# Six of eight modulation blocks summed over input tiles on VectorE, ScalarE and GpSimd instead of TensorE

## The chip, the cores and the metric

The kernel runs on one core of a Trainium2 chip. The time is that of the device for one execution, in microseconds; the median of several runs counts. The engines are TensorE (PE in the profile, PEld its weight loads), VectorE (DVE), ScalarE (ACT) and GpSimd (POOL); SyncE (SP) issues most DMAs. Each engine works through a queue of its own in order, and they wait for each other by semaphores.

## The reference

Two layers over a latent stream `x` (1024 tokens x 1024) and a context `ctx` (256 tokens x 1024): a windowed attention with sinks and rotary positions, then a bidirectional state-space mixer. Ahead of each mixer the stream is normalized and modulated, behind it the result is gated. What the change touches is where shift, scale and gate come from:

```python
def adaln(cond, w, b):
    mod = jax.nn.silu(cond) @ w + b
    return jnp.split(mod, 3, axis=-1)

for i in range(DEPTH):                       # 2 layers
    shift, scale, gate = adaln(c, w_ada[i], b_ada[i])
    shift_c, scale_c, gate_c = adaln(c_ctx, w_ada[i], b_ada[i])
    u = rms_normalize(h) * (1.0 + scale[:, None]) + shift[:, None]
    ...
    h = h + gate[:, None] * y
```

For each layer this is a product of two rows (c and c_ctx after silu) of length 1024 with a matrix of 1024 x 3072, plus a bias. All data are float32.

## The kernel before

**Modulation.** The matrix of a layer is cut into six column blocks of 512 (blocks 0 and 1 shift, 2 and 3 scale, 4 and 5 gate), and each block into eight input tiles of 128 rows, 128 x 512 in SBUF. Blocks 0 to 3 of layer 0 are needed at once and come first (`ada0`, L361). The eight others, (0,4), (0,5) and (1,0) to (1,5), are needed only later. `adaln_col` (L172) makes nine steps of each: step k loads tile k (L181, buffers `wh` and `wl` of the pool wv, four each); steps 3 and 7 add four float32 matmuls (L185) with 32 output columns each, one to each quarter of the PSUM tile `aps`. The weights `cs` hold the two rows in columns 0 and 1, zeros in the other 30, so partitions 32j and 32j + 1 hold the partial sums of the tiles j and 4 + j. The ninth step copies the PSUM tile to SBUF (L189) and calls `modulation` (L196): four matmuls against `sel`, two columns (L201), add up the four quarters and turn the row of 512 into four columns of 128 partitions; VectorE adds the bias (L203) into the tile `mod`. A float32 matmul is carried out in two passes, so the profile counts twice the instructions.

**The stage around it.** `qkvg` (L551) projects the modulated stream to k, v, q and g. Each product is done in three matmuls, with the operands split into a high part and a low part (`mm3`, L223, matmuls at L227 to L229). First come k and v for the three token tiles `TT` (512, 512 and 256 tokens), then eight column tiles x of wq, then eight of wg. For each x two halves of the weights (128 x 512) are loaded into `wr` (seven buffers, L220), split by ScalarE into `wh` (L213) and by VectorE into `wl` (L215), four buffers each, so the split runs one x ahead. Then follow the projections of the context tile (24 matmuls of 256 columns) and of the first latent tile (24 of 512); for the first four x of wg the latent tile was done earlier, and only the context tile is left. Results land in one of four PSUM tiles `pj`. q goes through `rope` (L496): VectorE reads PSUM twice (L501, L502), GpSimd multiplies by the sine (L503), VectorE adds (L504), ScalarE and VectorE split the sum (L522, L523) and SyncE stores it; the context tile of q is split from PSUM (L525, L526). g is read by ScalarE (L541) and VectorE (L542).

**What sets the order.** After each projection `fill` runs two or three of the 72 modulation steps, in the order in which the program is written:

```python
n = [3, 3, 3, 2]
for x in range(8):
    w = self.load_halves(a["wq"][x])
    for i in (2, 0):
        self.q_step(p, w, x, i)
        fill(n[x % 2 * 2 + (i == 0)])
```

The framework schedules the instructions of each engine from there by a time estimate of its own; the queues that result are fixed when the program is built. Behind the stage its pools are closed, and `attention` (L686) takes their memory; it interleaves the attention of the blocks with what is left of the projections. The gate of layer 0 is read in the output projection there (L724), the blocks of layer 1 later.

Of the kernel before, what the change touches and what calls it, by code (L numbers as in the profile page):

```python
# [17 lines left out]
P = 128  # L18
D = 1024
KT = D // P  # L20
# [22 lines left out]
    pj=1, S=2, pt=2, pv=1,  # L43
# [14 lines left out]
POST = 0.5  # L58
LATE = 3.0
DTLATE = (10.0, 13.0)  # L60
SEGS = (1.5, 2.0, 2.0, 2.2, 2.2)
_STOP = None

# [40 lines left out]
class Kernel:  # L104
# [52 lines left out]
    def load_cond(self, p):  # L157
        nc, t, cp = self.nc, self.t, self.cp
        cc = t(p, [P, KT, 2], F32, "cc")
        nc.sync.dma_start(cc, self.a["cc"].rearrange("p (k c) -> p k c", k=KT))  # L160
        th = t(p, [P, KT, 2], F32, "cth")
        nc.scalar.activation(th, cc, AF.Tanh, scale=0.5)
        nc.vector.tensor_scalar_mul(cc, cc, 0.5)
        cs = self.csf = t(cp, [P, KT, 2], F32, "cs")
        nc.vector.scalar_tensor_tensor(cs, in0=th, scalar=1.0, in1=cc, op0=ALU.add, op1=ALU.mult)

        self.sel = t(cp, [P, 2], F32, "sel")
        nc.vector.tensor_reduce(self.sel, self.ident.rearrange("p (j r) -> p r j", r=32)[:, 0:2], axis=mybir.AxisListType.X, op=ALU.add)
        self.bada = t(cp, [P, 2, 24], F32, "bada")
        nc.sync.dma_start(self.bada, self.a["bada"].rearrange("p (l t) -> p l t", l=2))  # L170

    def adaln_col(self, layer, n, pool, ps):  # L172

        nc, t = self.nc, self.t
        st = {}

        def step(k):
            if k == 0:
                st["ps"] = t(ps, [P, 512], F32, "aps", 2)
            raw = t(pool, [P, 4, P], F32, ("wh", "wl")[k // 4])  # L180
            nc.sync.dma_start(raw, self.a["w_ada"][layer, n, k].rearrange("p (a c) -> p a c", a=4))  # L181
            st[k] = raw
            if k % 4 == 3:
                for j in range(4):
                    nc.tensor.matmul(st["ps"][32 * j : 32 * j + 32], self.cs[:, k - 3 + j, :], st[k - 3 + j].rearrange("p a c -> p (a c)"), start=k == 3, stop=k == KT - 1)  # L185

        def fin():
            row = t(self.pq, [P, 512], F32, "qf")
            nc.scalar.copy(row, st["ps"])  # L189
            m = self.modulation(layer, n, row, ps)  # L190
            if n // 2 == 2 and layer == 0:
                nc.vector.tensor_scalar_mul(m, m, 0.5)

        return [lambda k=k: step(k) for k in range(KT)] + [fin]

    def modulation(self, layer, n, row, ps):  # L196

        nc = self.nc
        mt = self.t(ps, [P, 512], F32, "pt")
        for j in range(4):  # L200
            self.last_mod = nc.tensor.matmul(mt[:, 2 * j : 2 * j + 2], row[:, j * P : (j + 1) * P], self.sel, start=True, stop=True)  # L201
# [96 lines left out]
    def layer0(self):  # L298
        nc, t, a = self.nc, self.t, self.a
        cps = ExitStack()  # L300
        BUFS.update(S=1, pj=4, wr=7, qf=2, ql=2, wh=4, wl=4, sqt=2)
        self.psA = self.pool("psA", space=PSUM, ctx=cps)
        NB = (LAT + CTX) // P
        self.uH, self.uL = [None] * 3, [None] * 3
        cw = ExitStack()
        wvp = self.pool("wv", ctx=cw)

        self.cs = t(wvp, [P, KT, 32], F32, "cs32")
        nc.vector.memset(self.cs, 0.0)
        nc.vector.tensor_copy(self.cs[:, :, 0:2], self.csf)  # L310
# [12 lines left out]
        self.mask = t(kvp, [P, 1152], BF16, "mask")  # L323
        self.nsink = t(kvp, [P, HEADS], F32, "nsink")
        self.sink = t(kvp, [P, HEADS], F32, "sink")
        self.qkvg(p, wk, wv, wvp)
        if "u" in self.dump:
            for i, (s, n) in enumerate(TT):
                self.dump_split("u", self.uH[i], self.uL[i], i, n, s)
        cw.close()  # L330
        cps.close()
        with ExitStack() as c1:
            BUFS.update(S=2, pj=1)
            self.psA = self.pool("psT", space=PSUM, ctx=c1)
            self.attention(c1, ckv)
            BUFS.update(pj=2)
# [24 lines left out]
    def ada0(self, n, raw, ps):  # L361

        nc, t = self.nc, self.t
        pj = t(ps, [P, 512], F32, "aps", 2)
        for k in range(KT):
            j = k % 4
            mm = nc.tensor.matmul(pj[32 * j : 32 * j + 32], self.cs[:, k, :], raw[k // 2][:, k % 2], start=k < 4, stop=k >= 4)
# [128 lines left out]
    def rope(self, pool, ps, i, out):  # L496
        nc = self.nc
        s, n = TT[i]
        b = self.t(pool, [P, 512], F32, "rope_b")
        s -= self.rope_o  # L500
        nc.vector.tensor_mul(out, ps, self.cos[:, s : s + n])  # L501
        nc.vector.stream_shuffle(b, ps, mask=[(j + 16) % 32 for j in range(32)])  # L502
        nc.gpsimd.tensor_tensor(b, b, self.sin[:, s : s + n], op=ALU.mult)  # L503
        nc.vector.tensor_add(out, out, b)  # L504

    def load_rope(self, p, s, n):
        self.rope_o = s
        self.cos = self.t(p, [P, n], F32, "cos")
        self.sin = self.t(p, [P, n], F32, "sin")
        self.nc.sync.dma_start(self.cos, self.a["cos"][:, s : s + n])  # L510
        self.nc.sync.dma_start(self.sin, self.a["sin"][:, s : s + n])

    def qk(self, p, pj, i, l=None):
        nc, t = self.nc, self.t
# [36 lines left out]
    def qkvg(self, p, wk, wv, wvp):  # L551
        nc, t, a = self.nc, self.t, self.a
        ps = self.psA
# [3 lines left out]
        v = self.v  # L557
# [21 lines left out]
        for i, (s, n) in enumerate(TT):  # L579
# [22 lines left out]
        for x in range(8):  # L602
            w = self.load_halves(a["wg"][x])
# [354 lines left out]
    def dt_tail(self, raw, post):  # L958
# [153 lines left out]
    def ssd(self, c0):  # L1112
# [194 lines left out]
        with ExitStack():  # L1307
            for g in range(G):
# [321 lines left out]
```

## Time and profile before

| | us |
|---|---|
| median of 3 runs | 1850.06 (1848.47 to 1850.49) |
| the profiled execution | 1852.09 |
| its span, first to last instruction | 1850.4 |
| TensorE busy in the span | 1764.7 (95%) |
| VectorE, ScalarE, GpSimd busy | 1171.9, 894.8, 803.8 |
| first and last L185 matmul of the eight blocks | 142.6, 264.3 |

The last g matmul of the stage starts at 273.9 us, and attention follows. A matmul's row shows its own duration; since matmuls overlap in the array, the distance from one start to the next is what it costs the queue. Where rows are quoted, the columns of the timeline are start, duration, engine, line, operation, tiles (output<-inputs), shape, count and, in brackets, the idle time before with what ended it; the columns of a group are count, busy time, mean duration in ns and the idle time before. A row by line gives the shortest, median and longest duration in ns, and the first and last start.

### The profile page before, as it was taken

How to read it: one execution, taken by the hardware profiler on the slowest of the kernel's cores; microseconds unless marked ns; L12 is line 12 of the kernel's file. 1: busy time of each engine (PE TensorE's matmuls, PEld its weight loads, DVE VectorE, ACT ScalarE, POOL GpSimd, SP SyncE). 2: the span in 40 equal slices, each digit the busy share in tenths (PEclk: the TensorE clock that was granted, in tenths of full speed). 3: DMA queues.
4: the chain of work that ended last, by engine and by line, in shares of the span. 5: the costliest groups of instructions: out<-in, count | busy, mean ns of one | idle time of the engine just before them, and what ended most of it. 6: DMA issues, size and time to landing. Idle time of an engine off the chain costs nothing. (4 is left out here: it accounts for less than half of the span.)

```text
span 1850.4 us, 29176 instructions
## 1 busy us (share of the span) xinstructions
PE 1764.7 (95%) x10375; PEld 1506.2 (81%) x10375; DVE 1171.9 (63%) x2144; ACT 894.8 (48%) x1963; POOL 803.8 (43%) x1066
## 2 busy tenths in 40 slices
PE   6899998899999999989999999999999999999997
PEld 2697776788889687768889898988989898888886
DVE  4534426887777755684776757676675767766643
ACT  3812226677778765573443535344353534454422
POOL 2331107654456454202454554545455454554321
PEclk8999999999999999999999999999999999999998
DMA  8658856553355455321332333332232323455542
GB/s 313 233 135 254 250 160 150 132 124 88 95 129 131 105 147 169 127 67 43 83 74 78 81 77 78 80 89 69 77 93 65 86 72 99 150 170 166 177 137 69
DMA packets 212498, 227.64 MB, mean 123 GB/s; under 512 B 16384, under 2 KB 149632, under 8 KB 212352
## 3 DMA queue, kind: packets, MB, share of 16 engines
q1 hardware_dynamic: 178288, 207.12, 37.7%
q0 software_dynamic: 34064, 18.65, 5.6%
q8 instruction: 82, 1.34, 0.3%
q14 instruction: 64, 0.52, 0.1%
HBM read 190.88 MB, written 35.13 MB: 122 GB/s over the span
## 5 line engine op out<-in xcount | busy, mean ns | idle before, releaser
L227 PE MATMUL pj<-uH,wh 128*128 128x512 f32 (+1 forms) x712 | 257.7, 363 | 18.4 <-ACT uH L446 8.5
L228 PE MATMUL pj<-uL,wh 128*128 128x512 f32 (+1 forms) x712 | 244.9, 344 | 0.2 <-DVE uL L447 0.2
L229 PE MATMUL pj<-uH,wl 128*128 128x512 f32 (+1 forms) x712 | 244.2, 344 | 0.7 <-POOL wl L215 0.5
L1140 POOL TENSOR_TENSOR xw<-xn,dtdec 128x256 f32<-128x256 f32 x144 | 106.3, 741 | 197.2 <-PE psD L1165 125.0
L227 PEld LDWEIGHTS pj<-uH,wh 128*128 128x128 f32 x712 | 136.4, 192 | 48.1 <-issue 10.3
L1071 PE MATMUL pj<-uH,wh 128*128 128x512 f32 x512 | 165.6, 399 | 4.4 <-ACT bn L1025 2.4
L1071 PE MATMUL pj<-uL,wh 128*128 128x512 f32 x512 | 167.8, 401 | 1.1 <-DVE uL L291 1.1
L1071 PE MATMUL pj<-uH,wl 128*128 128x512 f32 x512 | 167.2, 401 | 0.7 <-DVE wl L1002 0.7
L215 POOL TENSOR_TENSOR wl<-wr,wh 128x512 fp32r<-128x512 f32 x92 | 123.0, 1341 | 88.3 <-ACT wh L213 87.8
L666 DVE TENSOR_TENSOR pl<-pt,ph 128x512 fp32r<-128x512 f32 x168 | 114.4, 687 | 66.3 <-ACT ph L665 65.5
L1096 PE MATMUL pj<-wh,uH 128*128 128x256 f32 x512 | 151.0, 295 | 2.6 <-ACT xn L1025 2.6
L228 PEld LDWEIGHTS pj<-uL,wh 128*128 128x128 f32 x712 | 137.0, 192 | 15.9 <-DVE uL L447 2.5
L229 PEld LDWEIGHTS pj<-uH,wl 128*128 128x128 f32 x712 | 135.9, 191 | 17.1 <-POOL wl L215 2.0
L1096 PE MATMUL pj<-wh,uL 128*128 128x256 f32 x512 | 149.1, 291 | 0.0
L1096 PE MATMUL pj<-wl,uH 128*128 128x256 f32 x512 | 146.4, 286 | 0.0
L213 ACT CAST wh<-wr 128x512 fp32r<-128x512 f32 (+1 forms) x132 | 84.7, 645 | 115.7 <-PE pj L228 83.2
L640 DVE CUSTOM_DVE_ANT_0 sm<-S,mask,nsink 128x640 f32<-128x640 f32 (+2 forms) x160 | 119.2, 771 | 21.4 <-PE S L637 13.6
L665 ACT CAST ph<-pt 128x512 fp32r<-128x512 f32 x168 | 97.4, 585 | 58.9 <-PE pt L661 55.3
L642 ACT ACTIVATE sm<-sm,nm 128x640 f32<-128x640 f32 (+2 forms) x160 | 118.7, 742 | 12.4 <-DVE nm L640 12.0
L1071 PEld LDWEIGHTS pj<-uH,wh 128*128 128x128 f32 x512 | 94.7, 189 | 25.0 <-ACT bn L1025 2.6
L1071 PEld LDWEIGHTS pj<-uL,wh 128*128 128x128 f32 x512 | 96.6, 189 | 21.9 <-DVE uL L291 2.0
L1071 PEld LDWEIGHTS pj<-uH,wl 128*128 128x128 f32 x512 | 96.4, 189 | 20.5 <-DVE wl L1002 1.1
(370 smaller groups left out, 4821.8 us busy)
## 6 DMA issues: line engine op xcount, KB each, us to landing
wr<-w_x SPq DMA_DIRECT2D x32, 512.0 KB, 5.2
M<-acs SPq DMA_DIRECT2D x64, 256.0 KB, 5.1
bw<-acs SPq DMA_DIRECT2D x64, 256.0 KB, 5.0
wr<-wo SPq DMA_DIRECT2D x48, 256.0 KB, 2.7
wr<-w_sk SPq DMA_DIRECT2D x24, 512.0 KB, 4.5
wr<-wg SPq DMA_DIRECT2D x40, 256.0 KB, 3.7
qs<-q POOLq DMA_DIRECT2D x40, 256.0 KB, 3.8
wada<-w_ada SPq DMA_DIRECT2D x16, 512.0 KB, 7.4
```

Source lines behind the costliest of these rows:

```text
L213: nc.scalar.copy(h, raw)
L215: (eng or nc.vector).tensor_tensor(l, raw, h, op=ALU.subtract)
L227: self.nc.tensor.matmul(ps, lh, rh, start=first and i == 0, stop=False)
L228: self.nc.tensor.matmul(ps, lh, rl, start=False, stop=False)
L229: self.nc.tensor.matmul(ps, ll, rh, start=False, stop=last and i == n - 1)
L640: nc.vector.tensor_tensor_reduce(out=sm[:, :W], in0=Sv, in1=self.mask[:, m0 : m0 + W], scale=-SCALE, scalar=self.nsink[:, 4 * j + r : 4 * ...
L642: nc.scalar.activation(sm[:, :W], sm[:, :W], AF.Exp, bias=nm[:, r : r + 1], scale=-1.0, accum_out=sums[:, r : r + 1])
L665: nc.scalar.copy(ph, ptf)
L666: nc.vector.tensor_sub(pl, ptf, ph)
L1071: nc.tensor.matmul(raw[:, 512 * i : 512 * i + 512], l[:, k, :], r[i][:, k, :], start=k + y == 0, stop=k == KT - 1 and y == 2)
L1096: nc.tensor.matmul(pj[:, c], l, r[:, k, :], start=c % 2 + q + k + y == 0, stop=c % 2 == 1 and q == 1 and k == 3 and y == 2)
L1140: nc.gpsimd.tensor_tensor(xw, X(st, c).rearrange("p (r h) -> p r h", r=R), self.dtdec[:, c, hd(d, g)].unsqueeze(2).broadcast_to([P, R, HP] ...
```

## The change

Six of the eight blocks, (0,4), (0,5) and (1,0) to (1,3), are summed over their eight input tiles by other engines: for row 0 VectorE computes `acc0 = tile * c0 + acc0` with c0 a value per partition; for row 1 ScalarE multiplies the tile in place by c1 and GpSimd adds it to `acc1`. What is left for TensorE is the sum over the 128 partitions: four matmuls of 256 columns for a block against `pick`, a tile of zeros with a column of ones, which puts the result of block i at partition 32g + i of one PSUM tile for all six. The other two, (1,4) and (1,5), stay on TensorE, and share a PSUM tile too: their place in it is set by where the window of 32 columns is put on `cs`, now 34 wide. At the end each of the two PSUM tiles is copied and turned once (24 and 4 columns), instead of one turn for each block.

The order of the blocks is one sum, one whole, five sums, one whole. There are 72 steps, as before: step s loads tile s, uses tile s - 2, and adds the total of a block four steps after its last use; the last two turn. The tiles load into six buffers: the four `wl`, and the second halves of the rope tables, which are now loaded as two halves each (`cos0`, `cos1`, `sin0`, `sin1`) and whose second halves are free once k is projected. The four `wh` hold two pairs of accumulators. The rest of the kernel is the same in the program; the scheduler's order differs from there to about 130 us into the attention.

```diff
-        self.sel = t(cp, [P, 2], F32, "sel")
+        self.sel = t(cp, [P, 4], F32, "sel")
...
-    def adaln_col(self, layer, n, pool, ps):
+    def ada1(self, p, ps):
...
+        sums = [(0, 4), (0, 5), (1, 0), (1, 1), (1, 2), (1, 3)]
+        whole = [(1, 4), (1, 5)]
+        order = [sums[0], whole[0]] + sums[1:] + [whole[1]]
+        raws, acc = {}, {}
+        aps = [t(ps, [P, 512], F32, "aps", 2) for _ in range(2)]
...
+        def load(s):
+            y, k = divmod(s, KT)
+            layer, n = order[y]
+            r = s % 6
+            raws[s] = t(p, [P, 512], F32, "wl") if r < 4 else t(self.pq, [P, 512], F32, ("cos1", "sin1")[r - 4])
+            nc.sync.dma_start(raws[s], self.a["w_ada"][layer, n, k])
+
+        def use(s):
+            y, k = divmod(s, KT)
+            x = order[y]
+            if x in whole:
+                if k % 4 == 3:
+                    i = whole.index(x)
+                    for j in reversed(range(4)):
+                        nc.tensor.matmul(aps[1][32 * j : 32 * j + 32], self.cs[:, k - 3 + j, 2 - 2 * i : 34 - 2 * i], raws.pop(s - 3 + j), start=i == 0 and k == 3, stop=i == 1 and k == KT - 1)
+                return
+            raw = raws.pop(s)
+            c0, c1 = self.csf[:, k, 0:1], self.csf[:, k, 1:2]
             if k == 0:
+                acc[x] = [t(p, [P, 512], F32, "wh") for _ in range(2)]
+                nc.vector.tensor_scalar(out=acc[x][0], in0=raw, scalar1=c0, scalar2=None, op0=ALU.mult)
+                nc.scalar.activation(acc[x][1], raw, AF.Copy, scale=c1)
+            else:
+                nc.vector.scalar_tensor_tensor(acc[x][0], in0=raw, scalar=c0, in1=acc[x][0], op0=ALU.mult, op1=ALU.add)
+                nc.scalar.activation(raw, raw, AF.Copy, scale=c1)
+                nc.gpsimd.tensor_tensor(acc[x][1], acc[x][1], raw, op=ALU.add)
+
+        def total(x):
+            i = sums.index(x)
+            a = acc.pop(x)
+            for g in reversed(range(4)):
+                nc.tensor.matmul(aps[0][32 * g : 32 * g + 32, :256], self.pick[:, 5 - i : 37 - i], a[g // 2][:, g % 2 * 256 : g % 2 * 256 + 256], start=i == 0, stop=i == 5)
+
+        def turn(b, w):
+            row = t(self.pq, [P, 512], F32, "qf")[:, :w]
+            nc.scalar.copy(row, aps[b][:, :w])
+            m = mt[b] = t(ps, [P, 512], F32, "pt")
+            sel = self.sel if b else self.ident.rearrange("p (g r) -> p g r", r=32)[:, :, 0:6]
+            n = 4 if b else 24
+            for j in range(w // P):
+                nc.tensor.matmul(m[:, n * j : n * j + n], row[:, j * P : (j + 1) * P], sel, start=True, stop=True)
...
+        def step(s):
+            if s < 8 * KT:
+                load(s)
+            if 0 <= s - LOOK < 8 * KT:
+                use(s - LOOK)
+            y, k = divmod(s - LOOK - LAGS, KT)
+            if k == KT - 1 and y >= 0 and order[y] in sums:
+                total(order[y])
+
+        steps = [lambda s=s: step(s) for s in range(8 * KT + LOOK + LAGS)]
+        return steps + [fin_sums, fin_whole]
...
-        self.cs = t(wvp, [P, KT, 32], F32, "cs32")
+        self.cs = t(wvp, [P, KT, 34], F32, "cs34")
...
+        self.pick = t(wvp, [P, 37], F32, "pick")
...
     def load_rope(self, p, s, n):
...
+        for h in range(n // 512):
+            for table, name in ((self.cos, "cos"), (self.sin, "sin")):
+                table.append(self.t(p, [P, 512], F32, f"{name}{h}"))
+                self.nc.sync.dma_start(table[h], self.a[name][:, s + 512 * h : s + 512 * h + 512])
...
-        ada = []
-        for layer, n in [(0, 4), (0, 5)] + [(1, n) for n in range(6)]:
-            ada += self.adaln_col(layer, n, wvp, ps)
+        ada = self.ada1(wvp, ps)
```

`LOOK` is 2 and `LAGS` is 4. `fin_sums` and `fin_whole` turn the two tiles and add the biases on VectorE.

More of the change, by code (lines that the diff above doesn't have):

```diff
@@ L60 @@
 DTLATE = (10.0, 13.0)
+LOOK = 2
+LAGS = 4
 SEGS = (1.5, 2.0, 2.0, 2.2, 2.2)
@@ L170, in load_cond, with fin_whole, fin_sums @@
         nc.sync.dma_start(self.bada, self.a["bada"].rearrange("p (l t) -> p l t", l=2))
-    def adaln_col(self, layer, n, pool, ps):
+    def ada1(self, p, ps):
         nc, t = self.nc, self.t
-        st = {}
-        def step(k):
-            if k == 0:
[L179 to L194, printed above, removed]
+        sums = [(0, 4), (0, 5), (1, 0), (1, 1), (1, 2), (1, 3)]
[3 more added lines that the diff above has]
+        aps = [t(ps, [P, 512], F32, "aps", 2) for _ in range(2)]
+        mt = {}
+        def load(s):
[15 more added lines that the diff above has]
+            c0, c1 = self.csf[:, k, 0:1], self.csf[:, k, 1:2]
+            if k == 0:
+                acc[x] = [t(p, [P, 512], F32, "wh") for _ in range(2)]
[18 more added lines that the diff above has]
+                nc.tensor.matmul(m[:, n * j : n * j + n], row[:, j * P : (j + 1) * P], sel, start=True, stop=True)
+        def fin_whole():
+            turn(1, 512)
+            nc.vector.tensor_tensor(self.mod[1][:, 16:24].rearrange("p (n j) c -> p n j c", j=4), mt[1][:, :16].rearrange("p (j n c) -> p n j c", n=2, c=2),
+                                    self.bada[:, 1, 16:24].rearrange("p (n j) -> p n j", j=4).unsqueeze(3).broadcast_to([P, 2, 4, 2]), op=ALU.add)
+        def fin_sums():
+            turn(0, 256)
+            v = mt[0][:, :48].rearrange("p (j c h n) -> p c n h j", j=2, c=2, h=2)
+            for layer, n0, n1, i in ((0, 4, 6, 0), (1, 0, 4, 2)):
+                for c in range(2):
+                    nc.vector.tensor_tensor(self.mod[layer].rearrange("p (n h j) c -> p c n h j", h=2, j=2)[:, c, n0:n1], v[:, c, i : i + n1 - n0],
+                                            self.bada[:, layer, 4 * n0 : 4 * n1].rearrange("p (n h j) -> p n h j", h=2, j=2), op=ALU.add)
+            nc.vector.tensor_scalar_mul(self.mod[0][:, 16:24], self.mod[0][:, 16:24], 0.5)
+            nc.vector.tensor_scalar_add(self.mod[1][:, 8:16], self.mod[1][:, 8:16], 1.0)
+        def step(s):
[8 more added lines that the diff above has]
+        return steps + [fin_sums, fin_whole]
@@ L200, in modulation @@
         for j in range(4):
-            self.last_mod = nc.tensor.matmul(mt[:, 2 * j : 2 * j + 2], row[:, j * P : (j + 1) * P], self.sel, start=True, stop=True)
+            self.last_mod = nc.tensor.matmul(mt[:, 2 * j : 2 * j + 2], row[:, j * P : (j + 1) * P], self.sel[:, :2], start=True, stop=True)
         m = self.mod[layer][:, n * 4 : n * 4 + 4, :]
@@ L366, in ada0 @@
             j = k % 4
-            mm = nc.tensor.matmul(pj[32 * j : 32 * j + 32], self.cs[:, k, :], raw[k // 2][:, k % 2], start=k < 4, stop=k >= 4)
+            mm = nc.tensor.matmul(pj[32 * j : 32 * j + 32], self.cs[:, k, 2:34], raw[k // 2][:, k % 2], start=k < 4, stop=k >= 4)
         row = t(self.p0, [P, 512], F32, "arow")
```

17 lines of the change are left out of this document (9 added, 8 removed).

## The prediction

> **What bounds the kernel now.** I read the page first, then the busy time in windows of the projection stage, the groups of the lines that the change touches, and the timeline of TensorE around one of them.
>
> ```profile
> span 1850.4 us, 29176 instructions
> PE 1764.7 (95%) x10375; PEld 1506.2 (81%) x10375; DVE 1171.9 (63%) x2144; ACT 894.8 (48%) x1963; POOL 803.8 (43%) x1066
> ```
> ```profile
> core 0: us, PE busy (x) PEld busy (x) DVE busy (x) ACT busy (x) POOL busy (x), PEclk, DMA share, GB/s
> 130.00:150.00 20.00, 20.00 (x135) 16.57 (x134) 5.77 (x12) 3.84 (x8) 4.80 (x8) 1.00 0.90 268
> ...
> 210.00:230.00 20.00, 20.00 (x142) 15.24 (x135) 10.21 (x20) 7.76 (x15) 1.57 (x1) 1.00 0.87 262
> ...
> 250.00:270.00 20.00, 20.00 (x121) 15.36 (x120) 4.33 (x10) 3.73 (x8) 2.81 (x4) 1.00 0.36 78
> ```
> All eight blocks are computed here, between 134 and 274 us, among the q and g projections. TensorE is busy the whole of every window at clock 1.00, VectorE about half or less, GpSimd less than a quarter: TensorE's queue sets this stage's length, and every microsecond taken from it would come off the end, if nothing else becomes late. The profiled execution took 1852.09 us (span 1850.4 and 1.7 around it), 2.0 over the median of the runs, 1850.06; differences below are applied to the median.
>
> **The change, part by part. What TensorE loses.**
> ```profile
> L185 PE MATMUL aps<-wh,cs x64: 592/605/617, 142.6 to 254.8; 128*32 128x512 f32 x64
> L185 PE MATMUL aps<-wl,cs x64: 592/605/617, 146.7 to 264.3; 128*32 128x512 f32 x64
> L201 PE MATMUL pt<-sel,qf x64: 165/251/272, 152.8 to 268.7; 128*128 128x2 f32 x64
> ```
> ```profile
> 134.17 0.28 PE L227 MATMUL pj<-uH,wh 128*128 128x256 f32 x1
> ...
> 141.61 0.39 PE L229 MATMUL pj<-uH,wl 128*128 128x512 f32 x1
> 141.84 0.39 PE L227 MATMUL pj<-uH,wh 128*128 128x512 f32 x1
> ...
> 142.29 0.39 PE L229 MATMUL pj<-uH,wl 128*128 128x512 f32 x1
> 142.61 1.07 PE L185 MATMUL aps<-wh,cs 128*32 128x512 f32 x8
> 143.61 0.39 PE L227 MATMUL pj<-uH,wh 128*128 128x256 f32 x1
> 143.83 0.28 PE L228 MATMUL pj<-uL,wh 128*128 128x256 f32 x1
> 143.95 0.29 PE L229 MATMUL pj<-uH,wl 128*128 128x256 f32 x1
> ...
> 152.58 0.39 PE L227 MATMUL pj<-uH,wh 128*128 128x512 f32 x1
> 152.81 0.95 PE L201 MATMUL pt<-sel,qf 128*128 128x2 f32 x8
> 153.62 0.49 PE L228 MATMUL pj<-uL,wh 128*128 128x512 f32 x1
> 153.94 0.40 PE L229 MATMUL pj<-uH,wl 128*128 128x512 f32 x1
> ```
> Matmuls overlap, so I price by starts. A 512-wide projection matmul starts 0.228 us after the one before, a 256-wide one 0.12. Without the group of eight, the second 256-wide one would start at 142.29 + 0.228 + 0.12 = 142.64; it starts at 143.83. So one group of four column blocks (two passes each) costs **1.19 us**, and there are 16. A turn: L229 starts 1.36 after L227 instead of 0.456, so **0.91**, eight times. Together 16 x 1.19 + 8 x 0.91 = 26.3 us.
>
> What is added: four groups for the two whole blocks, 4.8; six totals, half as wide. No row has that width; they lie between half a group, 0.6, and a whole one, 1.19. In a group the second pass follows about 1.07 - 0.605 = 0.465 after the first, so half the width saves about 0.43: I take 0.76, 4.6 in all. Two turns, one of them half as long: 0.9 + 0.5. Sum 10.8. TensorE alone: **26.3 - 10.8 = 15.5 us less.**
>
> **What the other engines gain.** 48 VectorE operations of 128x512 (42 with both tensors in SBUF), 48 on ScalarE, 42 adds on GpSimd.
> ```profile
> L215 POOL TENSOR_TENSOR wl<-wr,wh 128x512 fp32r<-128x512 f32 x92 | 123.0, 1341 | 88.3 <-ACT wh L213 87.8
> L732 POOL TENSOR_TENSOR sqa<-sqa,ut 128x512 f32<-128x512 f32 x7 | 9.1, 1296 | 0.0
> L542 DVE SCALAR_TENSOR_TENSOR qf<-qf,pj 128x512 f32<-128x512 f32 x14 | 9.6, 684 | 14.3 <-ACT qf L541 14.3
> L213 ACT CAST wh<-wr 128x512 fp32r<-128x512 f32 x124 | 76.4, 619 | 90.8 <-PE pj L228 66.9 <-DMA wr<-wo 7.7 <-DMA wr<-wq 5.9
> L289 ACT ACTIVATE h1k<-h1k,mod 128x512 f32<-128x512 f32 x8 | 6.3, 811 | 0.2 <-DVE h1k L288 0.2
> ```
> By busy time there is room on each: 42 x 1.30 = 55 us of GpSimd, 48 x 0.69 = 33 of VectorE, 48 x 0.62 to 0.81 = 30 to 39 of ScalarE, in 120 us. But GpSimd and VectorE don't run beside each other when both read two SBUF tensors:
> ```profile
> 143.97 0.67 DVE L215 TENSOR_TENSOR wl<-wr,wh 128x512 fp32r<-128x512 f32 x1
> 144.22 1.56 POOL L503 TENSOR_TENSOR rope_b<-rope_b,sin 128x512 f32<-128x512 f32 x1 [8.82 <-DVE rope_b L502]
> ...
> 218.02 1.57 POOL L503 TENSOR_TENSOR rope_b<-rope_b,sin 128x512 f32<-128x512 f32 x1 [8.86 <-DMA wh<-w_ada]
> ```
> ```profile
> 743.21 1.30 POOL L215 TENSOR_TENSOR wl<-wr,wh 128x512 fp32r<-128x512 f32 x1 [1.42 <-ACT wh L213]
> 743.27 1.79 DVE L291 TENSOR_TENSOR uL<-h,uH 128x512 fp32r<-128x512 f32 x1
> ```
> In the first pair VectorE is first and ends at 144.64; GpSimd ends at 145.78, 1.14 later. In the second GpSimd is first and ends at 744.51; VectorE ends at 745.06, 0.55 later, after 1.79 instead of 0.68. They take turns, and a turn costs **0.55 for VectorE and 1.14 for GpSimd, 1.69 a pair**. The Trainium skill (SBUF — State Buffer, section "SBUF: two separate sides") says that the shared port pair is an exclusive lock, held for the whole instruction. Where it differs is the size: whole instructions would be 0.69 + 1.30 = 1.99 a pair, while the rows show that about 0.3 of each pair overlaps. By the page's wording the sum below would come out near the upper end.
>
> **The sum.** The built order (the order of each queue as the scheduler left it, without times) puts the sums' VectorE operations among the wl splits (L215) that TensorE needs. VectorE runs in order, so the wl of a projection waits for all sums ahead of it. The last one that matters is the wl of the fifth g projection (g4): 41 of the 42 two-tensor sums stand ahead of it. From the first sum to there the shared turns are 41 pairs x 1.69 = 69.3, 22 wl and 16 rope and ql operations x 0.55 = 20.9 and 8 rope products x 1.14 = 9.1: **99 us**. The first sum can start at about 138: the wl buffers that its tile loads into come free as the last v projections end, just ahead of 134.17, and a load takes 4.8:
> ```profile
> wl<-w_ada SPq DMA_DIRECT2D x32, 256.0 KB, 4.8
> ```
> TensorE alone would come to g4 at 134.2 + 8 x 8.35 (a q projection: 24 x 0.12 + 24 x 0.228) + 4 x 2.9 + about 6 = 218.6 us; now it does at 134.2 + 66.8 + 11.5 + 56 of 72 steps of the 26.3 = 233. The turns need until 138 + 99 = 237 without any gap. They have a gap: the second block is a whole one, so between the second and the fourth q projection there is little for them to do, and VectorE's order can't pass the reads of a projection's PSUM (L501) there. Going through the built order projection by projection (start of the next = the later of TensorE's end and the second wl less 1.4, as the second half of the weights is needed only then) with 5 sums, 4 other operations and a rope product to a q projection, 11.8 us against TensorE's 8.9: the lead of one projection that the four wl buffers give is used up at q7 (wl at 196.9, TensorE at 197.3); then g0 waits 3.2, g1 3.1, g2 1.6, g3 8.4 and g4 5.9. g4 starts at 240.9 instead of 233. From there 33.4 us of projections are left and 4.5 of the new groups (before 5.9 of the old): the stage ends at 278.8. The same arithmetic for the kernel before gives 272.2 (its last g matmul starts at 273.9):
> ```profile
> 273.94 0.39 PE L229 MATMUL pj<-uH,wl 128*128 128x512 f32 x1
> ```
> So **+6.6 us** with perfect turns. The ends of this price: at no cost of the lock, -15.5; with whole instructions, the same walk gives 295.5, +23. I take the turns, since the rows are of just these shapes. To this comes the clock after idle time:
> ```profile
> 280.00:285.00 5.00, 1.41 (x6) 0.66 (x5) 1.78 (x8) 0.29 (x1) 1.90 (x4) 0.77 1.50 270
> 285.00:290.00 5.00, 4.27 (x18) 3.69 (x19) 2.10 (x6) 4.47 (x13) 2.71 (x3) 0.55 0.58 96
> ```
> After 3.6 us of idle TensorE the clock granted was 0.55 over the next 5 us, some 2 us lost. The waits ahead of g3 and g4 would bring that once on the path: +2. Total +8.6, **1859 us**.
>
> **Edits that I cost at nothing.** The 64 weight loads have the same size and queue; they are freed by GpSimd instead of TensorE, and a late add holds SyncE, with the next weight loads behind it. The seven wr tiles, three and a half projections ahead, cover some 29 us of q projections; without them g0 to g3 would wait longer still. The rope tables come in halves, long before use. The totals wait for GpSimd's last add, but stand four steps (some 6 us) behind it. The small adds at the end are fewer and their result is not read before the output projection. The order of attention's first 130 us is shuffled by the scheduler, of the same instructions; I price it at 0 with some 3 us to either side. Nothing moves from layer 1 on.
>
> **Rivals.** **(B) TensorE stays the bound:** the lock costs less than its rows, or VectorE's order slips past it; then -15.5, **1834.5**, faster. It decides at a pair cost: 5 pairs and 3.3 us of the rest fit into the 8.9 of a q projection only under 1.1 us a pair, against 1.69 in the rows. For it speaks the spare busy time of all engines; against it all the pairs above, and the g projections (2.9 us each with 2 to 5 pairs). **(C) The turns pack:** the gap of the whole block is used and the wait at g4 is 237 - 1.4 instead of 240.9; the end is then at 273 to 274, **1850 to 1852**, no change. Against it: VectorE's order holds the third block's sums behind a read of PSUM. **(D) More than turns:** the chain tile landed, VectorE, ScalarE (in place), GpSimd, free, is 4.8 + 0.7 + 0.7 + 1.3 = 7.5 us without any wait, for six tiles; with waits of a turn at each link it becomes as slow as the port, and the pair costs its 1.99: **1873**.
>
> **How the numbers follow.** Chances: forecast 0.62 (its own range 1852 to 1868), B 0.10, C 0.18, D 0.10. Faster by over 0.2% (3.7 us, about what a measurement of this kernel tells from no change): B and a sixth of C, 0.13; within: the rest of C (0.15) and a little of the forecast (0.02); slower: the rest, 0.70. The range goes from 1843, which leaves out B, to 1874, which takes in D.
>
> **What would show it.** Right: the sums' two-tensor operations on VectorE average over 1.0 us instead of 0.69, and GpSimd's adds over 1.4; TensorE idle 15 us or more between 205 and 250, put to DVE wl; the totals and groups on TensorE at 10 to 11 us; the granted clock under 1.00 in that stretch. Wrong: TensorE busy throughout, the last g projection near 258 (B), or the waits spread over the q projections from the start (D). Waits for tiles or on SyncE ahead of wr would mean that the loads, not the port, decide.

## The result, and the profile after

The changed kernel takes **1876.53 us** (median of 4 runs, 1873.5 to 1877.78) against 1850.12: a ratio of **1.0136, 95% interval 1.012 to 1.0153**. The forecast was 1859 with 1874 as the upper end, so the sign is right and the size is not: slower by 26 us instead of 9.

The profiled execution took 1876.86 us. Its page begins:

```profile
span 1874.8 us, 29189 instructions
PE 1762.3 (94%) x10275; PEld 1509.9 (81%) x10275; DVE 1239.9 (66%) x2189; ACT 921.9 (49%) x2005; POOL 866.8 (46%) x1108
```

TensorE is busy 2.4 us less than before over the whole span, and the span is 24.4 us longer. Busy time in windows of the projection stage (columns: window, its length, then TensorE, its weight loads, VectorE, ScalarE, GpSimd, the clock granted, the DMA engines' share, GB/s):

```profile
130.00:150.00 20.00, 20.00 (x124) 16.88 (x122) 15.76 (x16) 7.90 (x14) 12.38 (x9) 1.00 0.54 164
150.00:170.00 20.00, 15.91 (x85) 12.06 (x82) 10.52 (x19) 5.61 (x13) 4.59 (x4) 0.91 0.77 220
170.00:190.00 20.00, 17.42 (x105) 14.66 (x104) 18.89 (x20) 9.15 (x15) 13.21 (x10) 1.00 0.69 223
190.00:210.00 20.00, 12.38 (x71) 10.45 (x69) 18.76 (x22) 7.65 (x13) 13.41 (x9) 0.89 0.74 206
210.00:230.00 20.00, 16.51 (x89) 13.44 (x89) 19.26 (x24) 9.70 (x18) 12.95 (x10) 0.76 0.67 187
230.00:250.00 20.00, 12.92 (x66) 11.11 (x66) 19.07 (x22) 9.69 (x16) 13.16 (x9) 0.67 0.65 195
250.00:270.00 20.00, 16.46 (x90) 13.01 (x91) 10.91 (x12) 7.35 (x13) 8.28 (x7) 0.83 0.75 233
```

From 170 to 250 us VectorE is occupied 76 of 80 us, TensorE has gaps, and from 190 on the granted clock falls to 0.67. What TensorE waited for in the stage:

```profile
PE aps L216 <- POOL wh L210: 12.4, 4, 7.7
PE pj L285 <- ACT wh L271: 6.3, 2, 3.9
PE pj L287 <- DVE wl L273: 6.1, 4, 2.8
PE aps L199 <- DMA wl<-w_ada: 3.7, 1, 3.7
```

28.5 us of waits in eleven pieces, by (columns) total, times, longest. The clock comes on top. I estimate its cost as busy time times the part not granted: over the rows above 1.4 + 1.4 + 4.0 + 4.3 + 2.8 = 13.8 us.

Why VectorE is full can be read from the groups of its operations in the stage, and from VectorE's and GpSimd's timelines around 210 us:

```profile
L208 DVE SCALAR_TENSOR_TENSOR wh<-wl,cs,wh 128x512 f32<-128x512 f32 x28 | 31.8, 1137 | 2.2 <-DMA wl<-w_ada 2.0
L273 DVE TENSOR_TENSOR wl<-wr,wh 128x512 fp32r<-128x512 f32 x25 | 28.2, 1128 | 2.6 <-ACT wh L271 2.6
```
```profile
208.95 1.64 DVE L208 SCALAR_TENSOR_TENSOR wh<-sin,cs,wh 128x512 f32<-128x512 f32 x1
210.51 1.76 DVE L567 TENSOR_TENSOR qf<-qf,rope_b 128x512 f32<-128x512 f32 x1
212.19 1.77 DVE L208 SCALAR_TENSOR_TENSOR wh<-wl,cs,wh 128x512 f32<-128x512 f32 x1
213.89 0.68 DVE L273 TENSOR_TENSOR wl<-wr,wh 128x512 fp32r<-128x512 f32 x1
```
```profile
208.33 1.71 POOL L210 TENSOR_TENSOR wh<-wh,wl 128x512 f32<-128x512 f32 x1
210.00 1.72 POOL L210 TENSOR_TENSOR wh<-wh,cos 128x512 f32<-128x512 f32 x1
211.80 1.62 POOL L210 TENSOR_TENSOR wh<-wh,sin 128x512 f32<-128x512 f32 x1
```

```profile
L210 POOL TENSOR_TENSOR wh<-wh,wl 128x512 f32<-128x512 f32 x28 | 43.1, 1542 | 23.9 <-ACT wl L209 23.0
```

The last row is GpSimd's group of adds. Three GpSimd adds and three VectorE operations run in step, one pair every 1.56 to 1.80 us. The wl split at 213.89 starts when the last of these adds is through (213.42) and takes 0.68.

**How the kernels are compared below.** The whole time mixes the stage with what lies around it, so I cut each trace at two marks: VectorE's last rope of k and the first score matmul of attention. In the timelines of before and of after:

```profile
111.34 0.69 DVE L501 TENSOR_TENSOR qf<-pj,cos 128x512 f32<-128x512 f32 x1 [4.09 <-PE pj L229]
...
274.17 0.28 PE L637 MATMUL S<-kHH,qs 128*128 128x256 f32 x1
```
```profile
106.83 0.69 DVE L564 TENSOR_TENSOR qf<-pj,cos 128x512 f32<-128x512 f32 x1 [4.25 <-PE pj L287]
...
294.66 0.38 PE L699 MATMUL S<-kHH,qs 128*128 128x256 f32 x1
```

Between the marks lies the stage: 162.8 us before, 187.8 after, +25.0. Each stage is read from one profiled execution. Before and e3, which differ in the rope tables only, both have 162.8, but no kernel was profiled twice, so differences of 2 to 4 us between stages rest on little. Ratios are to the kernel before in runs on the same chip; the runs of before spread from 1842 to 1858 us there.

| kernel | stage, us | ratio of times [95% interval] |
|---|---|---|
| before | 162.8 | 1 |
| after | 187.8 | 1.0136 [1.012, 1.0153] |
| e1_psum_acc | 165.3 | 1.0005 [0.9991, 1.0019] |
| e2_no_add | 161.8 | 0.999 [0.9973, 1.0007] |
| e3_rope_halves | 162.8 | 0.9992 [0.998, 1.0005] |
| e4_turn_only | 156.7 | 0.9932 [0.9918, 0.9946] |
| e5_lag8 | 188.9 | 1.0152 [1.0124, 1.0179] |
| e6_spread | 180.0 | 1.0113 [1.0086, 1.014] |
| e7_psum_spread | 163.0 | 1.0002 [0.9985, 1.002] |
| e8_no_sums | 157.4 | 0.9978 [0.9961, 0.9995] |
| e9_no_loads | 144.6 | 0.9925 [0.9905, 0.9946] |
| e10_act_queue | 160.1 | 0.9979 [0.9963, 0.9995] |
| e11_two_sums | 166.8 | 1.0012 [0.9996, 1.0028] |
| e12_small_loads | 153.4 | 0.9965 [0.9949, 0.998] |
| e13_grouped | 154.5 | 0.9942 [0.9922, 0.9963] |
| e14_two_sums_grouped | 155.7 | 0.9967 [0.995, 0.9984] |

### The profile page after: what moved, and what is told of

It reads as the page before. It is cut to its first block, busy times and chain, and to the rows that moved or that the text cites. A ratio compares the mean times of both kernels' runs of the same rounds, so it can differ in the third digit from the quotient of the medians.

```text
span 1874.8 us, 29189 instructions
## 1 busy us (share of the span) xinstructions
PE 1762.3 (94%) x10275; PEld 1509.9 (81%) x10275; DVE 1239.9 (66%) x2189; ACT 921.9 (49%) x2005; POOL 866.8 (46%) x1108
## 5 line engine op out<-in xcount | busy, mean ns | idle before, releaser
L285 PE MATMUL pj<-uH,wh 128*128 128x512 f32 (+1 forms) x712 | 262.4, 370 | 14.2 <-ACT wh L271 6.3
L287 PE MATMUL pj<-uH,wl 128*128 128x512 f32 (+1 forms) x712 | 250.2, 352 | 6.7 <-DVE wl L273 6.1
L286 PE MATMUL pj<-uL,wh 128*128 128x512 f32 (+1 forms) x712 | 250.1, 352 | 0.2 <-DVE uL L508 0.2
L285 PEld LDWEIGHTS pj<-uH,wh 128*128 128x128 f32 x712 | 140.9, 198 | 36.9 <-ACT wh L271 9.9
L287 PEld LDWEIGHTS pj<-uH,wl 128*128 128x128 f32 x712 | 140.2, 197 | 26.4 <-DVE wl L273 7.5
L704 ACT ACTIVATE sm<-sm,nm 128x640 f32<-128x640 f32 (+2 forms) x160 | 118.6, 742 | 12.4 <-DVE nm L702 12.2
L1133 PEld LDWEIGHTS pj<-uH,wh 128*128 128x128 f32 x512 | 94.1, 188 | 25.0 <-ACT bn L1087 2.8
L1133 PEld LDWEIGHTS pj<-uH,wl 128*128 128x128 f32 x512 | 96.1, 188 | 20.4 <-DVE wl L1064 1.1
```

What stands on the lines that cost most here:

```text
L285: self.nc.tensor.matmul(ps, lh, rh, start=first and i == 0, stop=False)
L286: self.nc.tensor.matmul(ps, lh, rl, start=False, stop=False)
L287: self.nc.tensor.matmul(ps, ll, rh, start=False, stop=last and i == n - 1)
L704: nc.scalar.activation(sm[:, :W], sm[:, :W], AF.Exp, bias=nm[:, r : r + 1], scale=-1.0, accum_out=sums[:, r : r + 1])
L1133: nc.tensor.matmul(raw[:, 512 * i : 512 * i + 512], l[:, k, :], r[i][:, k, :], start=k + y == 0, stop=k == KT - 1 and y == 2)
```

## The experiments

### The lock: sums in PSUM (e1), and no adds (e2)

```diff
-                acc[x] = [t(p, [P, 512], F32, "wh") for _ in range(2)]
+                acc[x] = [t(ps, [P, 512], F32, "pt"), t(p, [P, 512], F32, "wh")]
...
+            if k == KT - 1:
+                s0 = t(p, [P, 512], F32, "wh")
+                nc.scalar.copy(s0, acc[x][0])
+                acc[x][0] = s0
```

> The changed kernel, but VectorE's running sum of each block stands in PSUM (a free pt bank) instead of SBUF, and ScalarE copies it to SBUF once at the block's end (6 copies of about 0.6 us). The number, size and order of VectorE's and GpSimd's operations stay; VectorE's sums read only one tensor from SBUF. Theory (the lock between VectorE's sums and GpSimd's adds makes both too slow for TensorE): the sums go from 1.71 us median back to about 0.7, GpSimd's adds from 1.61 to about 1.3, nearly all of TensorE's 28 us of waiting goes, the clock with it, and the time is 1833 to 1845. Rival 1 (loads and the hand-over of tiles from DMA to VectorE, ScalarE, GpSimd and back set the pace): the sums are short but the waits stay, 1868 to 1880. Rival 2 (VectorE has simply too much work ahead of the wl splits): as rival 1 for half of it, 1860 to 1870. Rival 3 (the totals stand too early in TensorE's order, whatever the lock): the 12.4 us on totals stay, 1855 to 1862.

Of the kernel with the sums in PSUM, the groups of VectorE and GpSimd in the stage, and TensorE's waits there:

```profile
L208 DVE SCALAR_TENSOR_TENSOR pt<-wl,cs,pt 128x512 f32<-128x512 f32 x28 | 21.0, 749 | 4.1 <-DMA wl<-w_ada 3.6
L210 POOL TENSOR_TENSOR wh<-wh,wl 128x512 f32<-128x512 f32 x28 | 40.4, 1443 | 17.3 <-ACT wl L209 16.3
```
```profile
PE aps L220 <- POOL wh L210: 9.5, 3, 3.8
PE pj L289 <- ACT wh L275: 2.0, 2, 1.2
```

The same 28 sums go from 1137 to 749 ns; the stage drops by 22.5 us. Nothing was left out (six copies on ScalarE come on top). The edit also frees SBUF accumulators, but in the changed kernel no operation waited for one. So the shared access is the cause of those 22.5. The Trainium skill (SBUF — State Buffer, section "SBUF: two separate sides") lets a VectorE operation contend when it has two SBUF inputs; the trace agrees, 749 ns with one. But the time is 1852, above the 1845 expected, 12.8 us of waits are left, and the adds only fall from 1542 to 1443 ns, since they still meet the wl splits. Without the lock on the sums the stage is still no shorter than before.

In e2 the line of GpSimd's add is removed.

> The changed kernel without GpSimd's 42 adds: the second row of the six summed blocks (the context's) holds only its first tile. Loads, ScalarE's scaling and VectorE's sums with both tensors in SBUF stay. Theory (the lock): VectorE's sums at about 0.7 us without a partner, no wait on the totals, TensorE-bound: 1832 to 1842. Rival 1 (loads and tiles): a link of the chain goes, some 5 us better, 1868 to 1874. Rival 2 (VectorE's own work): 1865 to 1877. Rival 3 (totals too early for GpSimd's last add): the totals wait no more, 12 us and some of the clock come back, 1855 to 1862.

Its waits:

```profile
PE pj L284 <- ACT wh L270: 6.7, 4, 2.8
PE pj L286 <- DVE wl L272: 3.5, 5, 1.5
```

26.0 us of stage go with the adds, and the waits on the totals with them. The theory expected 1842 at most; it was 1849. Something holds the stage that is neither GpSimd's adds nor their lock.

### The placing: later totals (e5), other dealing (e6), both without the lock (e7)

```diff
-LAGS = 4
+LAGS = 8
```

> The changed kernel with the totals placed eight steps behind their last add instead of four. The stage is read from the last rope of k to the first score matmul of attention: 162.9 us before, 187.9 in the changed kernel. If the totals' waits are a loss of their own (a bad place in TensorE's order): their 12.4 us and some 5 of the 12 lost to the clock come back, stage about 171, time 1857 to 1862. Theory (VectorE and GpSimd together are slower than TensorE, and the totals are only the place where TensorE meets it): the totals' waits go and the waits on wl and wh grow by nearly as much, stage 182 to 187, time 1870 to 1877.

```profile
PE pj L287 <- DVE wl L273: 14.2, 7, 3.7
PE pj L285 <- ACT wh L271: 9.8, 3, 5.0
```

As the theory said: the totals wait no more, and the waits on wl and wh grow from 12.4 to 24.0 us. The stage, 188.9, and the time, 1877.2, lie just above its ranges. The totals are a place, not a cause.

```diff
-        n = [3, 3, 3, 2]
+        n = [2, 4, 2, 4]
```

> The changed kernel with its steps dealt out by TensorE's time: 2 behind a 256-wide projection and 4 behind a 512-wide one instead of 3, 3, 3, 2, so 2 instead of 3 in each of g0 to g3 (2.9 us each) and 6 instead of 5.5 in a q projection (8.9 us). If what is too fast is the dealing (three tiles in 2.9 us), the stage drops by 8 to 15 us, 1861 to 1868. If the shared port sets the pace everywhere (about 1.7 us a pair, 5.5 pairs and other work already longer than a q projection), it drops by less than 5 us, 1871 to 1877.

In the profile the stage is 7.8 us shorter, at the edge of the first case, and the time, 1870.9, falls between the two; the ratio's interval overlaps that of the changed kernel. The dealing may account for a few microseconds; this is not settled.

e7 joins the edits of e1, e5 and e6.

> VectorE's sums in PSUM, the totals eight steps behind and the steps dealt out by TensorE's time, all three together. If the lock, the totals' place and the dealing are the whole loss, TensorE is the bound: stage 147 to 151 (162.9 less 15.6, and some), 1834 to 1840. If GpSimd's own adds (42 x 1.3 us and the 28 wl splits that still share the port) are too slow for the pace, the stage stays at 156 or above, 1844 to 1852.

Stage 163.0, 2.3 less than e1, and no gain in time. The wait on the totals falls to 1.6 us, while one wait of 6.7 us on ScalarE's wh appears, and one of 2.9 on a w_ada tile. This is in the second case, but GpSimd isn't the one waited for. The next runs look for what is.

### The floor: no sums (e8), no loads for them (e9), issues elsewhere (e10), small loads (e12)

```diff
-            else:
-                nc.vector.scalar_tensor_tensor(acc[x][0], in0=raw, ...
-                nc.scalar.activation(raw, raw, AF.Copy, scale=c1)
-                nc.gpsimd.tensor_tensor(acc[x][1], acc[x][1], raw, op=ALU.add)
```

> The changed kernel with each summed block holding only its first tile: 42 VectorE sums, 42 ScalarE scalings and 42 GpSimd adds are left out, with the loads, the first tiles, the totals, the two whole blocks and both turns kept. This is TensorE's share of the change alone. If the 15.5 us of the prediction are right: stage 147 to 148, time 1833 to 1837. If totals and turns cost TensorE more than 10.8 us: above 150 and 1838. In the kernel without the adds TensorE still waited 14 us on wl and wh between 208 and 233; if VectorE's sums caused that, it is gone here; if the loads did, it stays.

The stage is 157.4, not 147. TensorE's waits, ScalarE's between 180 and 240 us, and SyncE's queue (start, issue time, line, transfer, count):

```profile
PE pj L281 <- ACT wh L267: 7.7, 4, 5.2
PE pj L283 <- DVE wl L269: 1.5, 3, 1.0
ACT wh L267 <- DMA wr<-wg: 17.6, 7, 4.1
```
```profile
196.82 0.67 SPq L274 DMA_DIRECT2D wr<-wg  x1
...
199.66 0.43 SPq L274 DMA_DIRECT2D wr<-wg  x1
200.19 0.45 SPq L594 DMA_DIRECT2D q<-qh  x1
...
204.82 0.59 SPq L595 DMA_DIRECT2D q<-ql  x1
205.46 0.58 SPq L274 DMA_DIRECT2D wr<-wg  x1
...
207.53 0.90 SPq L274 DMA_DIRECT2D wr<-wg  x2
```

Between the second and the third of these g weight loads stand eight stores of q, 5.3 us of SyncE. From 196.82 to 208.43 it issues 19 transfers, about 0.5 us each, 9.8 us of 11.6. Before 196.82 it had issued one g weight load, at 160.01; in the kernel before, SyncE had issued seven by 198.82, the first at 173.59. In the changed kernel, with the sums, ScalarE waited for a g weight only once, 1.1 us.

e9 adds to this:

```diff
+            if order[y] not in whole and k:
+                return
             r = s % 6
```

> As the kernel without the sums, and the 42 tiles that nothing reads there any more aren't loaded either (42 of the 64 loads of 256 KB and their issues on SyncE are left out). In the kernel without sums TensorE still waited 9 us, on ScalarE's wh, which waited for the g weights: they landed late while the DMA engines were 0.94 to 1.08 busy and SyncE issued 7 to 9 us in every 10. If the load stream is that third bound: waits gone, stage 147 to 149 (162.8 less 15.5), 1833 to 1838. If TensorE's own share is worth less than 15.5: stage 152 or more with no waits in it.

```profile
190.00:200.00 10.00, 10.00 (x65) 8.21 (x65) 5.93 (x10) 2.86 (x5) 2.94 (x2) 1.00 0.56 139
200.00:210.00 10.00, 10.00 (x65) 8.36 (x65) 6.49 (x11) 3.82 (x8) 1.57 (x1) 1.00 0.72 199
210.00:220.00 10.00, 10.00 (x89) 9.46 (x88) 5.78 (x11) 4.59 (x10) 0.00 (x0) 1.00 0.78 233
```

TensorE is busy throughout at clock 1.00, and the stage is 144.6: this is TensorE's share of the change alone, **18.2 us**. The whole time falls by less, 13.9 us [10.0, 17.6]. In the kernel without sums the 42 loads cost 12.8 of the 18.2.

```diff
-            nc.sync.dma_start(raws[s], ...
+            nc.scalar.dma_start(raws[s], ...
```

> The kernel without the sums, all 64 loads kept but issued from ScalarE's queue instead of SyncE's. If SyncE's issuing (some 0.5 us for each of 20 or more transfers in 10 us, and its waits for buffers in order, which hold the g weights behind them) is what makes the g weights late: the waits go, stage 147 to 151. If the transfer rate of the DMA engines is: the same bytes in less time, waits on wh stay, stage 155 to 158. If ScalarE is held by the loads' waits for free tiles: worse, stage above 160.

Inconclusive: 160.1, at the edge of the third case. The g weights are in time (1.0 us on wh), but TensorE waits 8.4 us for w_ada tiles of a whole block, whose loads are now issued in ScalarE's order. The wait has moved, not gone.

```diff
+            c = 512 if order[y] in whole or not k else 16
-            nc.sync.dma_start(raws[s], self.a["w_ada"][layer, n, k])
+            nc.sync.dma_start(raws[s][:, :c], self.a["w_ada"][layer, n, k, :, :c])
```

> The kernel without the sums, with all 64 loads issued from SyncE in their places, but each of the 42 tiles that nothing reads brings 16 columns (8 KB) instead of 512 (256 KB). If the bytes through the DMA engines hold the g weights back: as without these loads, stage 144 to 148, 1833 to 1838. If SyncE's issuing and its order do: as with the full loads, stage 155 to 158, 1844 to 1848, with waits on wh before g0 to g3.

Stage 153.4 and 1843.35, between the two cases: cutting the bytes gives 4.0 of the 12.8 back, and 8.8 stay with the transfers as such. This run doesn't tell their issues and place on SyncE from their packets on the DMA engines: a small load still brings 128 rows, and over 132 us around the stage the packets are as many (20281 in e8, 21036 here) for 20.82 instead of 30.53 MB. The times agree in order, 0.9925, 0.9965, 0.9978, though the last two intervals overlap. The Trainium skill (DMA: Bandwidth & Descriptors, section "Issuing engines are not separate DMA queues") says that issue time is usually small beside the transfer. The trace agrees on the single transfer (0.5 us of issue, and in e8 a landing 4.1 us after it for a w_ada tile, 5.2 for a g weight) and not on the sum: some twenty in 11.6 us leave the queue little room.

### The parts without sums (e3, e4, e13), and thin sums without GpSimd (e11, e14)

e3 is the kernel before with only the rope tables in halves.

> The kernel before, with only the rope tables in halves (four tiles of 128x512 and four loads instead of two of 128x1024). In the changed kernel the first rope starts 4.7 us earlier than before, ahead of everything that the change names. If the smaller loads bring that: first rope near 73.5 instead of 78.3 and 1845 to 1847. If it is the place of the tiles or an accident of the start: first rope at 78.3 and 1850, within 0.2%.

No effect: stage 162.8, 1850.59. The operation ahead of the first rope, which the two cases name, came at 75.5, between them; see the last section on that.

e4 is the kernel before, all blocks whole, with one bank and one turn:

```diff
-                    nc.tensor.matmul(st["ps"][32 * j : 32 * j + 32], self.cs[:, k - 3 + j, :], ..., start=k == 3, stop=k == KT - 1)
+                    nc.tensor.matmul(aps[32 * j : 32 * j + 32], self.cs[:, k - 3 + j, 14 - 2 * i : 46 - 2 * i], ..., start=i == 0 and k == 3, stop=i == 7 and k == KT - 1)
```

> The kernel before, with all eight blocks whole on TensorE as before, but collected in one PSUM bank (a window of the widened cs puts block i in rows 2i and 2i+1 of each group) and turned by one turn of 128x16 at the end instead of eight of 128x2; no sums on other engines, same loads. Seven turns of 0.91 us go: 6.4 us less, 1843 to 1845, if turns cost what the start times of the trace say. If a turn's cost is only its own busy time of 8 x 0.12 and hidden in the pipeline, within 0.2% of before. If attention's order is shuffled to a worse one, 1847 to 1850.

The stage is 6.1 us shorter, as worked out, and TensorE waits for nothing in it. The time is 1839.86: **faster than the kernel before**, by 0.68% [0.54, 0.82], and so than the changed one. That is some 12.6 us; the half beyond the stage lies in attention and the rest of that profile, and I have no cause for them.

e13 is e4 with `for j in reversed(range(4))`: the column block loaded last is issued first.

> The kernel with the shared turn only, and in each group of four the column block whose tile lands last is issued first, so that the four stand together in TensorE's order (16 groups of 4; before, 14 of 4 and the rest apart as 1, 1, 1, 2, 3). Each block that stands apart costs about 1.06 instead of 0.30 us, so 2 to 3 us less: stage 153 to 155 against 156.7, time ratio to before 0.991 to 0.993. If the group now waits for its last tile where single blocks could start, no gain: 156 to 158.

2.2 us off the stage as expected, but the ratio, 0.9942, is above the expected one, and the time is that of e4 within the intervals.

e11 is e4 with two blocks summed:

```diff
+            if i in sums:
...
+                for c in range(2):
...
+                        nc.vector.scalar_tensor_tensor(x, in0=st[k], scalar=f, in1=x, op0=ALU.mult, op1=ALU.add)
...
+                        nc.scalar.copy(s0, acc[i][c])
```

> From the kernel with the shared turn only: two of the eight blocks, well apart, are summed, both rows on VectorE into two free PSUM banks (32 operations of about 0.75 us, none on GpSimd), copied to SBUF by ScalarE and summed over the partitions by two matmuls of 128x512 each. TensorE loses four groups of 1.19 and gains two totals of about 0.7: 3.4 us less. If sums without a shared port and spread thinly fit beside the projections: stage 153 to 154 against 156.7, ratio to before 0.991. If VectorE's 24 us more delay wl or the rope reads even so: stage 157 to 162, ratio 0.994 to 0.997.

Ten microseconds longer than e4, beyond both cases, with TensorE busy throughout. Its timeline shows a column block by itself (two passes, x2) between projection matmuls:

```profile
198.17 0.39 PE L255 MATMUL pj<-uH,wl 128*128 128x512 f32 x1
198.49 1.04 PE L202 MATMUL aps<-wh,cs 128*32 128x512 f32 x2
199.46 0.50 PE L253 MATMUL pj<-uH,wh 128*128 128x512 f32 x1
```

L253 starts 1.29 after L255 instead of 0.23, so a lone block costs 1.06 us, where four together cost 1.19. The scheduler left 13 column blocks and three of the totals alone, 16 in all: 16 x 1.06 - 4 x 1.19 = 12 us. The Trainium skill (TensorEngine Tiling (Array Packing), section "Tiling Modes") says that a change of tiling mode drains TensorE; that fits, and the price is from these rows.

> Two of the eight blocks summed on VectorE into PSUM as in the run with two sums, but the groups of four of the other blocks stand together. If the lone column blocks were its loss (16 x 1.06 against 4 x 1.19 is 12 us): stage 151 to 155 against 166.8, ratio to before 0.990 to 0.993. If VectorE's 32 sums were: it stays above 160, ratio 0.998 to 1.002.

Grouped again, the stage is 155.7: the lone blocks were 11.1 us of e11. Beside e13 (154.5) the two sums bring nothing even here: in this run's windows VectorE is busy 10.00 of 10 us at 210 to 230. Neither expectation was met in full: 155.7 lies just above the first, and the ratio, 0.9967, between the two.

## Why the prediction was off

The stage came out +25.0 where the prediction summed to +8.6. In the prediction's own terms, as the changed kernel shows them (its waits ahead of g0 to g4 are the way from -15.5 to +6.6):

| term | predicted | shown | read from |
|---|---|---|---|
| TensorE sheds | -15.5 | -18.2 | e9 against before |
| TensorE's waits (the lock) | +22.1 | +28.5 | waits in the stage after |
| clock after idle | +2 | +13.8, an estimate | windows after |
| sum | +8.6 | +24.1 of +25.0 | |

The runs bear this balance out. e1 takes 15.7 us of waits away and, by the same estimate, 7.0 of the clock's cost: 22.7 where its stage drops by 22.5. By single edits the +25.0 divides as follows, in the order in which the runs add them (another order would split them differently):

| step | us | by |
|---|---|---|
| TensorE sheds | -18.2 | e9 against before |
| the 42 loads | +12.8 | e8 against e9 |
| VectorE's sums and ScalarE's scalings | +4.4 | e2 against e8 |
| the adds, lock included | +26.0 (22.5 of it the sums' lock) | after against e2; e1 |

- **The step that failed** is the clock term in "The sum": "The waits ahead of g3 and g4 would bring that once on the path: +2". The waits came in eleven pieces between 150 and 256 us, the granted clock lay at 0.67 to 0.91 in five of the seven windows, and the cost is 13.8. It follows from the waits: in e9, which has none, the clock is 1.00. The waits themselves were the second miss, 28.5 against 22.1; 3.7 of them are on a w_ada tile, which the sum had at nothing.
- **The mechanism was right:** pairs stand 1.56 to 1.80 us apart against 1.69, sums take 1137 ns and adds 1542 where over 1000 and over 1400 were named, TensorE was idle 15.6 us between 205 and 250. That taking the sums out of the lock brought 22.5, so near the 22.1 of the walk, is in part luck: some 7 of the 22.5 are the clock's, which the walk leaves out, and the adds still meet the wl splits. Rival D came nearest in time (1873) by a wrong mechanism: whole instructions, 1.99 a pair.
- **A floor that the prediction didn't have** lies in "Edits that I cost at nothing": "The 64 weight loads have the same size and queue", covered by the seven wr tiles. Without any sum the stage is 157.4 with them and 144.6 without 42 of them. So rival B's 1834.5 is out of reach even without a lock: with the sums, 1849 without adds and 1852 without their lock. In the changed kernel this floor lies behind the sums (1.1 us of waiting for g weights). Why the loads cost nothing before stays open: TensorE was slower then, but the loads also had eight buffers and another order on SyncE, and in e4 and e13 the stage is 6 to 8 us shorter with all 64 loads and ScalarE waits for no g weight.
- **What TensorE sheds** was 2.7 us too small. By start times in e9, the new groups, totals and turns cost 10.1 us against 10.8, a total 0.76 as reckoned. The rest was in the kernel before: two of its 16 groups don't stand together but on both sides of a turn.

```profile
187.60 0.28 PE L229 MATMUL pj<-uH,wl 128*128 128x256 f32 x1
187.81 1.04 PE L185 MATMUL aps<-wh,cs 128*32 128x512 f32 x2
188.79 1.05 PE L201 MATMUL pt<-sel,qf 128*128 128x2 f32 x8
189.77 1.06 PE L185 MATMUL aps<-wh,cs 128*32 128x512 f32 x6
...
191.10 0.39 PE L228 MATMUL pj<-uL,wh 128*128 128x512 f32 x1
```

Without group and turn the matmul at 191.10 would start at 187.60 + 0.12 + 0.228 = 187.95. So the two cost 3.15 us here instead of 1.19 + 0.91, and as much at the other such place (252.36). That adds 2.1 to the 26.3: 28.4 less 10.1 is 18.3.

- **VectorE's plain work** was taken as free below its average load. With ScalarE's scalings the sums cost +4.4 without a partner. In the stretch where they lie densely, g0 to g3, three sums, two wl splits and more fall on 2.9 us; that this is the cause isn't shown apart, and the intervals of e2 and e8 overlap.
- **The totals** were priced at nothing, as "four steps (some 6 us) behind" GpSimd. They waited 12.4 us; but moved to eight steps the loss stays (e5), so it isn't a term of its own.
- **The place of the waits** was half right. They fall between 150 and 256 us, the most from 200 on, but on the totals and wh as much as on wl.
- Outside the stage the prediction had 0. In the two profiled executions the start is 4.5 us earlier and what follows the stage 3.9 longer, which nearly cancel; in e1 and e5, with the same program there, what follows is 3.1 shorter and 0.1 longer than before, so I read no cause into it.

## What to carry to other kernels

- When work leaves the engine that sets the pace, the floor is not "old time less removed work": something else can bound the stage close below, here the weight loads. A kernel with the new work left out measures that floor directly, in one run.
- Price waits of TensorE together with the clock that they cost. By the estimate above, 28.5 us of waits in eleven pieces cost another 13.8 here.
- Moving reductions to VectorE and GpSimd together is worth less than their idle shares say when both read two SBUF operands; an accumulator in PSUM takes VectorE out of the conflict.
- Here the cheap part of the change (one shared bank, one turn) was the good one: with no sums at all it is faster than both kernels.

## What the runs showed of the hardware that I had not expected

**The start of the program varies.** The last rope of k comes at 106.8 to 108.8 us in some profiled executions and at 110.2 to 112.6 in others. After and e2 have the same program up to there and differ by 5.8 us. In the changed kernel and then in e2, around 24 us:

```profile
22.02 2.49 DVE L521 TENSOR_TENSOR uL<-uL,rr 128x512 f32<-128x512 f32 x4
23.39 6.29 POOL L273 TENSOR_TENSOR wl<-wr,wh 128x512 fp32r<-128x512 f32 x4 [6.43 <-ACT wh L271]
```
```profile
24.47 4.64 DVE L520 TENSOR_TENSOR uL<-uL,rr 128x512 f32<-128x512 f32 x4
25.24 6.21 POOL L272 TENSOR_TENSOR wl<-wr,wh 128x512 fp32r<-128x512 f32 x4 [7.46 <-ACT wh L270]
```

Where three of VectorE's four products have started when GpSimd's splits begin, they take 2.49 us; where they come 2.4 us later, they meet them and take 4.64. So the lock, as I read it, adds some 2.2 us to a shift of 2.4; where that shift and the rest of the 5.8 come from isn't shown.

**A lone 32-column block between full-width matmuls costs 1.06 us, four together 1.19**: most of its price goes with standing alone, not with its work. Set together again (e14), the blocks gave 11.1 us back.
